# The first product on x times g, scaled by token afterwards, and a new order of the first loads, in a two-layer mLSTM and attention trunk

## The chip, the cores and the metric

The kernel runs on one core of a Trainium2 chip. The metric is the device time of one execution in microseconds. Before the change three runs gave 887.74, 888.80 and 890.71 us, a median of 888.8.

## The reference

Two layers over 256 tokens of 1024 channels, all in float32. Each layer computes, with x the running sum:

```python
h = rmsnorm(x, norm_mix_g[l])           # x * rsqrt(mean(x*x) + eps) * g
x = x + mixer_block(h, w_in[l], ...)    # proj = h @ w_in, split into mqk, mv, mo, gates, aq, ak, av, ga, gb
h = rmsnorm(x, norm_mlp_g[l])
x = x + sqrelu_mlp(h, w_up[l], w_down[l])
```

and at the end one more rmsnorm. Every projection starts from the same normed h; mv, the values of the mLSTM branch, is one of them: `mv = rmsnorm(x, g) @ w_in[:, 1024:2048]`. The norm's factor belongs to a token (a row of x) and g to a channel (a column).

## The kernel before, in words

Tokens lie in two tiles of 128 (tt = 0, 1) and channels in two halves of 512 (hf = 0, 1) or eight groups of 128 (k = 0 to 7). X holds x with tokens on the partitions. A product needs x transposed, with channels on the partitions (hT), so x is normed, transposed on TensorE against `ident`, and evacuated from PSUM.

Every matrix operand is split in two: hi, a rounded copy made by ScalarE, and lo, the remainder, made by VectorE as the operand minus hi. Each product is then three matmuls: hi by hi, hi by lo, lo by hi (`xs` at lines 202 to 215 with 512 output columns, `ws` at 217 to 229 with 256).

**Weights.** They come as pieces of 128 rows by 1024 columns (512 KB), loaded by SP (`piece`, line 89; `kv_piece`, lines 98 and 99, takes two loads for a piece) into four `raw` buffers. `pump_hi` (line 142) makes hi on ScalarE, `pump_lo` (line 117) makes lo on VectorE, and behind each lo `pump_dma` issues the load of the piece four further on, which takes the buffer that this lo has finished with. SP works in order: a load that waits for its buffer holds up all loads behind it.

**Slots.** The work of TensorE is a list of slots, each a list of units (three matmuls, or a call). `run_slots` (line 182) goes through them and emits for each slot, in this order: the functions of `at`, hi of the pieces that the slot may reach ahead to (four ahead of its own, `AHEAD`, or fewer by `limits`), the functions of `at_late`, the matching lo, the functions of `at_last`, the units, and the functions of `after`. Each engine works through its own instructions in the order in which they are emitted; what runs early or late is thus fixed by where it is emitted.

**The start.** Slots 0 to 7 are the product mv (`s_mv` = 0): piece k is used in slot k in the second half, and in slots 0 to 3 the order is "t", token tile 0 for k = 0, 1, then 2, 3, then token tile 1. Slots 8 to 11 (`s_kv` = 8) are the keys, values and gates, from pieces 8 to 11. `mv_evac` (lines 588 to 594) empties mv's four PSUM banks after slot 7: banks (tt, 0) on ScalarE, banks (tt, 1) on VectorE. The next product's banks (kk for the keys, kv0 and kv1 for values and gates) are the same ones: in the trace the first matmul of kk waits for ScalarE's first evacuation and the first of kv1 for VectorE's first.

`setup_start` (line 391) issues the first loads, all from SP: x of tile 0 in halves (lines 393, 394), the row of g (395), pieces 0 to 2, x of tile 1 (398), piece 3, and then eleven small loads (`small_loads`, line 379: the bias table, and for each layer gate biases, sinks, and the rows of the convolution). Then it emits warm-up matmuls on zeros (`N_WARM`). `first_norm` (line 515) squares x (lines 333, 335), forms the factor r (line 339 on VectorE, the power on POOL at line 340), scales (523), transposes (528), and evacuates hi and lo with g as a factor per partition (532, 538). The rest of x is done by `tr_all` from within slots 1 and 2.

`setup_small` runs at the head of slot 2: mask and constants on POOL, `Rs` (line 424) and `sel` (line 428) on ScalarE. `setup_cols` runs at the head of slot 4: TensorE transposes the 80 rows of the convolution weights and biases (line 432) and the bias table (435), VectorE copies them to `cw` and `rbT` (433, 437), POOL spreads the bias table.

Of the kernel before, what the change touches and what calls it, by code (L numbers as in the profile page):

```python
# [42 lines left out]
def trunk(ctx: ExitStack, tc: tile.TileContext, x, norm_mix_g, w_in, conv_w, conv_b, b_igate, b_fgate,  # L43
# [60 lines left out]
    def pump_dma():  # L104
        j = n_dma[0]
        if j < len(pieces):
            raws[j] = wp.tile([P, 1040], F32, tag="raw", bufs=N_RAW, name=nm("raw"))
            pieces[j][0](raws[j])
            n_dma[0] += 1
# [3 lines left out]
    def pump_lo(eng=None):  # L113
# [5 lines left out]
        los.clear()  # L119

# [110 lines left out]
    def call(f):  # L231
        return ([], f)
# [144 lines left out]
    N_WARM = (26, 16, 8)  # L377

    def small_loads():
        S0["b8"] = big8()  # L380
        rows = S0["rows"] = S0["b8"][:80, 0, 0:P]
        rb = S0["rb"] = const.tile([NB_BUCKETS, 16], F32, name="rb")
        nc.sync.dma_start(rb, rel_bias)
        for l in range(DEPTH):
            nc.sync.dma_start(gb_bias[:, l, 0:4], b_igate[l].partition_broadcast(P))
            nc.sync.dma_start(gb_bias[:, l, 4:8], b_fgate[l].partition_broadcast(P))
            nc.sync.dma_start(sink[:, l, :], attn_sinks[l].partition_broadcast(P))
            nc.sync.dma_start(rows[40 * l : 40 * l + 32, :], conv_w[l].rearrange("j (m c) -> (j m) c", c=P))
            nc.sync.dma_start(rows[40 * l + 32 : 40 * l + 40, :], conv_b[l].rearrange("(m c) -> m c", c=P))

    def setup_start():
        grow = big8()[:8, 0, 0:P]
        nc.sync.dma_start(X[:, 0, 0:512], xv[:, 0, 0:512])
# [13 lines left out]
        pw = psA()  # L407
        for _ in range(N_WARM[0]):
            nc.tensor.matmul(pw[:, :P], mask, mask, start=True, stop=True)
        pg = psA()  # L410
        nc.tensor.transpose(pg[:, :8], grow, ident[:8, :8])
        S0["gcol"] = const.tile([P, KT], F32, name="gcol")
        S0["pg"], S0["pw"] = pg, pw
        for _ in range(N_WARM[1]):
            nc.tensor.matmul(pw[:, :P], mask, mask, start=True, stop=True)
# [99 lines left out]
    def first_norm(st, xtag, nxt):  # L515

        xh, xl = st["hT"] = xT_tiles(xtag)
        N = [Norm(0), Norm(1)]
        gcol, xn, pts = S0["gcol"], {}, {}

        def scale(tt, hf):
            xn[tt, hf] = tmp()
            nc.vector.tensor_scalar(xn[tt, hf], X[:, tt, hc(hf)], N[tt].r[:, :1], None, op0=ALU.mult)

        def tr(tt, hf):
            pts[tt, hf] = psB()
            for j in range(4):
                nc.tensor.transpose(pts[tt, hf][:, j * P : (j + 1) * P], xn[tt, hf][:, j * P : (j + 1) * P], ident)

        def hi(tt, ks):  # L530
            for k in ks:
                nc.scalar.activation(xh[:, k, tt * P : (tt + 1) * P], pts[tt, k // 4][:, k % 4 * P : (k % 4 + 1) * P],  # L532
                                     AF.Copy, scale=gcol[:, k : k + 1])

        def lo(tt, ks):
            for k in ks:
                s = slice(tt * P, (tt + 1) * P)
                nc.vector.scalar_tensor_tensor(xl[:, k, s], pts[tt, k // 4][:, k % 4 * P : (k % 4 + 1) * P],
# [562 lines left out]
```

## Time and profile before

| what | value |
|---|---|
| median of three runs | 888.8 us |
| the profiled execution, its own time | 888.86 us |
| its span, first to last instruction | 887.0 us |
| TensorE matmuls busy | 872.7 us of the span |
| VectorE busy | 573.1 us |
| ScalarE busy | 467.2 us |
| mean granted TensorE clock | 0.997 |
| data moved by DMA | 155.28 MB, 175 GB/s |

Times in the profile are microseconds from the start of the span. A row of the timeline gives start, duration, engine, line of the kernel, operation, what it writes and reads, and in square brackets how long the engine sat idle before it and who released it. PE is TensorE, PEld its weight loads, DVE VectorE, ACT ScalarE, POOL GpSimd; SPq is the queue from which SP issues loads. A row of a table of stretches gives the stretch, its length, the busy time of each engine with the count of instructions, the granted clock as a share of full speed, the share of the DMA engines' time, and GB/s. Rows of one tile give the count and the least, median and largest duration in nanoseconds.

### The profile page before, as it was taken

The numbers are of one execution on the slowest core, as the hardware profiler recorded it, in microseconds if no ns is written. First come the engines' busy times: TensorE is split into PE (matmuls) and PEld (weight loads), VectorE is DVE, ScalarE is ACT, GpSimd is POOL, SyncE is SP. The second block draws the span as 40 slices with busy tenths as digits, with TensorE's granted clock in tenths as the row PEclk, the third lists the DMA queues.
The fourth block names the chain that finished last, engine by engine and source line by source line (L and its number), as shares of the span: only waits on it lengthen the run. The fifth ranks groups of instructions, "written<-read, shape, count | busy, mean of one in ns | idle before, by whom it ended". The sixth has DMA issues, their size and how long they took to land.

```text
span 887.0 us, 14892 instructions
## 1 busy us (share of the span) xinstructions
PE 872.7 (98%) x5837; PEld 788.0 (89%) x5837; DVE 573.1 (65%) x922; ACT 467.2 (53%) x769; POOL 132.3 (15%) x166
## 2 busy tenths in 40 slices
PE   8999999999999999999999999999999999999996
PEld 6899889999988999998889988899998899999985
DVE  5758879666666664545564778876666765737362
ACT  5556776654445454545355448665543553636351
POOL 1362434120000000000002435321100000000000
PEclk9999999999999999999999999999999999999999
DMA  6874435445457647474655545354464467565621
GB/s 229 280 259 169 139 119 167 142 145 169 163 190 236 208 146 239 128 247 138 202 180 178 171 139 154 133 146 163 143 216 147 159 217 236 168 211 173 201 104 48
DMA packets 48663, 155.28 MB, mean 175 GB/s; under 512 B 7912, under 2 KB 10064, under 8 KB 48592
## 3 DMA queue, kind: packets, MB, share of 16 engines
q1 hardware_dynamic: 47408, 150.63, 52.8%
q0 software_dynamic: 896, 3.17, 1.1%
q8 instruction: 46, 0.75, 0.3%
q10 hardware_dynamic: 288, 0.52, 0.2%
q14 instruction: 25, 0.20, 0.1%
HBM read 153.23 MB, written 1.07 MB: 174 GB/s over the span
## 4 chain that ended last, share of the span: by engine, by line
PE 90%; DVE 4%; DMA 2%; issue 2%; ACT 1%; POOL 0%; SPq 0%; POOLq 0%; ACTq 0%
PE pa L211 13%; PE pa L212 13%; PE pa L213 13%; PE pa L226 9%; PE pa L225 9%; PE pa L227 9%; PE pb L226 5%; PE pb L225 5%; PE pb L227 5%; DMA raw<-in_w_in 2%; PE pb L841 1%; PE pb L861 1%; DVE lo L117 1%; PE pb L313 1%; PE pb L901 1%
## 5 line engine op out<-in xcount | busy, mean ns | idle before, releaser
L117 DVE TENSOR_TENSOR lo<-raw,hi 128x1024 fp32r<-128x1024 f32 (+1 forms) x274 | 329.4, 1224 | 143.8 <-ACT hi L142 140.8
L142 ACT CAST hi<-raw 128x1024 fp32r<-128x1024 f32 (+1 forms) x280 | 286.6, 1049 | 187.4 <-PE pa L213 51.7
L225 PE MATMUL pa<-xh,hi 128*128 128x256 f32 x800 | 228.9, 286 | 0.6 <-ACT vm L594 0.6
L226 PE MATMUL pa<-xl,hi 128*128 128x256 f32 x800 | 225.5, 282 | 0.0
L227 PE MATMUL pa<-xh,lo 128*128 128x256 f32 x800 | 224.4, 281 | 0.0
L211 PE MATMUL pa<-hi,xh 128*128 128x512 f32 (+1 forms) x416 | 162.6, 391 | 0.7 <-ACT xh L532 0.6
L212 PE MATMUL pa<-lo,xh 128*128 128x512 f32 (+1 forms) x416 | 160.8, 387 | 0.6 <-DVE lo L117 0.4
L213 PE MATMUL pa<-hi,xl 128*128 128x512 f32 (+1 forms) x416 | 160.4, 386 | 0.0
L225 PEld LDWEIGHTS pa<-xh,hi 128*128 128x128 f32 x800 | 151.3, 189 | 1.7 <-ACT vm L594 1.1
L226 PEld LDWEIGHTS pa<-xl,hi 128*128 128x128 f32 x800 | 151.6, 189 | 0.3
L227 PEld LDWEIGHTS pa<-xh,lo 128*128 128x128 f32 x800 | 151.7, 190 | 0.0
L225 PE MATMUL pb<-xh,hi 128*128 128x256 f32 x384 | 108.2, 282 | 0.0
L226 PE MATMUL pb<-xl,hi 128*128 128x256 f32 x384 | 107.6, 280 | 0.0
L227 PE MATMUL pb<-xh,lo 128*128 128x256 f32 x384 | 107.4, 280 | 0.0
L212 PEld LDWEIGHTS pa<-lo,xh 128*128 128x128 f32 x416 | 78.3, 188 | 16.7 <-DVE lo L117 1.6
L213 PEld LDWEIGHTS pa<-hi,xl 128*128 128x128 f32 x416 | 78.1, 188 | 16.8
L211 PEld LDWEIGHTS pa<-hi,xh 128*128 128x128 f32 x416 | 78.2, 188 | 15.9 <-ACT xh L532 0.8
L340 POOL TENSOR_TENSOR sm<-sm,mhalf 128x1 f32<-128x1 f32 x10 | 7.4, 744 | 504.8 <-DVE sm L339 504.8
L226 PEld LDWEIGHTS pb<-xl,hi 128*128 128x128 f32 x384 | 72.4, 188 | 1.8
L225 PEld LDWEIGHTS pb<-xh,hi 128*128 128x128 f32 x384 | 72.2, 188 | 1.8
L227 PEld LDWEIGHTS pb<-xh,lo 128*128 128x128 f32 x384 | 72.2, 188 | 0.0
L211 PE MATMUL pa<-hi,b 128*128 128x512 f32 x128 | 50.4, 394 | 0.0
(197 smaller groups left out, 990.9 us busy)
## 6 DMA issues: line engine op xcount, KB each, us to landing
raw<-in_w_in SPq DMA_DIRECT2D x104, 512.0 KB, 4.4
raw<-in_w_up SPq DMA_DIRECT2D x64, 512.0 KB, 5.0
raw<-in_w_down SPq DMA_DIRECT2D x64, 512.0 KB, 4.4
raw<-in_w_branch_a SPq DMA_DIRECT2D x16, 512.0 KB, 3.5
raw<-in_w_branch_m SPq DMA_DIRECT2D x16, 512.0 KB, 3.8
raw<-in_w_out SPq DMA_DIRECT2D x16, 512.0 KB, 4.5
b<-ed SPq DMA_DIRECT2D x4, 512.0 KB, 4.9
g<-in_mlstm_norm_g POOLq DMA_DIRECT2D x2, 512.0 KB, 5.4
```

The source lines that it names most:

```text
L117: (eng or nc.vector).tensor_tensor(lo[:, :n], raw[:, :n], hi[:, :n].bitcast(F32), op=ALU.subtract)
L142: nc.scalar.copy(hi[:, :n], raw[:, :n])
L211: nc.tensor.matmul(b, xh[:, kt, s], wh[:, c], start=first, stop=False)
L212: nc.tensor.matmul(b, xh[:, kt, s], wl[:, c], start=False, stop=False)
L213: nc.tensor.matmul(b, xl[:, kt, s], wh[:, c], start=False, stop=last)
L225: nc.tensor.matmul(o, wh[:, c], xh[:, kt, :], start=first and half == 0, stop=False, skip_group_check=True)
L226: nc.tensor.matmul(o, wh[:, c], xl[:, kt, :], start=False, stop=False, skip_group_check=True)
L227: nc.tensor.matmul(o, wl[:, c], xh[:, kt, :], start=False, stop=last, skip_group_check=True)
L313: nc.tensor.transpose(pt[:, j * P : (j + 1) * P], src[:, j * P : (j + 1) * P], ident)
L841: nc.tensor.transpose(tp[:, j * P : (j + 1) * P], L[:, j * P : (j + 1) * P], ident)
L861: nc.tensor.matmul(o, va[:, 0, vs], PT[:, 0:T], start=(h0 % 4 == 0), stop=False, skip_group_check=True)
L901: nc.tensor.matmul(pn[:, :257], W[:, tt * P : (tt + 1) * P], vm[:, 0, h, :], start=True, stop=(tt == 0))
```

## The change

- The first product mv of layer 0 takes x times g, not normed (`hU`, in the tiles `xb`), and `mv_evac` multiplies its result by r, the norm's factor of each token.
- x is transposed as it is; VectorE multiplies by g out of PSUM into a buffer `xg` (`times_g`), ScalarE copies to hi, VectorE forms lo. Half 0 of both token tiles is done ahead of slot 0, half 1 within slots 1 and 2 (`rest`), and there, behind it, the squares and r too.
- The normed x for all later products (`hT`) is made from `xg` in slots 5 and 6: r is spread over all partitions by two small matmuls (`rows`), and `normed` multiplies and splits, four channel groups at a time.
- First loads: the row of g and x of tile 1, half 0, are issued by ScalarE; pieces 0 and 1 come in two halves each; x's second halves come before pieces 2 and 3. Piece 0 is also split in halves on ScalarE (`pump_hi_part`).
- The small loads go from the start to the ends of the preparation of slots 1, 2 and 3 (`at_last`), and the two layers' loads are merged.
- Slots 0 to 3 are in order "k" (piece k in slot k), slot 0 with token tiles inside. `limits` now holds slots 0 and 1 only. The warm-up matmuls are 24 and 22.

```diff
     def piece(w, kt, c0):
-        def load(raw):
-            nc.sync.dma_start(raw[:, :1024], w[kt * P : (kt + 1) * P, c0 : c0 + 1024])
+        def load(raw, parts=1):
+            for a in range(0, 1024, 1024 // parts):
+                b = a + 1024 // parts
+                nc.sync.dma_start(raw[:, a:b], w[kt * P : (kt + 1) * P, c0 + a : c0 + b])
...
+    def pump_hi_part(a, b):
+        j = n_split[0] - (1 if a else 0)
+        if not a:
+            pc[j] = tuple(wp.tile([P, 1040], F32R, tag=t, bufs=N_SPL, name=nm(t)) for t in ("hi", "lo"))
+            los.append(j)
+            n_split[0] += 1
+        nc.scalar.copy(pc[j][0][:, a:b], raws[j][:, a:b])
...
-    N_WARM = (26, 16, 8)
+    N_WARM = (24, 22)
...
+    def small_loads(i):
+        if i == 0:
+            S0["b8"] = big8()
+            S0["rows"] = S0["b8"][:80, 0, 0:P]
+            rb = S0["rb"] = const.tile([NB_BUCKETS, 16], F32, name="rb")
+            nc.sync.dma_start(rb, rel_bias)
+            nc.sync.dma_start(S0["rows"][0:64, :], conv_w.rearrange("l j (m c) -> (l j m) c", c=P))
+        elif i == 1:
+            nc.sync.dma_start(S0["rows"][64:80, :], conv_b.rearrange("l (m c) -> (l m) c", c=P))
+            nc.sync.dma_start(sink, attn_sinks.partition_broadcast(P))
+        else:
+            nc.sync.dma_start(gb_bias[:, :, 0:4], b_igate.partition_broadcast(P))
+            nc.sync.dma_start(gb_bias[:, :, 4:8], b_fgate.partition_broadcast(P))
 
     def setup_start():
         grow = big8()[:8, 0, 0:P]
+        nc.scalar.dma_start(grow, norm_mix_g[0].rearrange("(k c) -> k c", c=P))
         nc.sync.dma_start(X[:, 0, 0:512], xv[:, 0, 0:512])
+        nc.scalar.dma_start(X[:, 1, 0:512], xv[:, 1, 0:512])
+        pump_dma(2)
+        pump_dma(2)
         nc.sync.dma_start(X[:, 0, 512:], xv[:, 0, 512:])
-        nc.sync.dma_start(grow, norm_mix_g[0].rearrange("(k c) -> k c", c=P))
-        for i in range(N_RAW):
-            if i == 3:
-                nc.sync.dma_start(X[:, 1, :], xv[:, 1, :])
-            pump_dma()
-        small_loads()
+        nc.sync.dma_start(X[:, 1, 512:], xv[:, 1, 512:])
+        pump_dma()
+        pump_dma()
...
     def first_norm(st, xtag, nxt):
...
+        uh, ul = st["hU"] = xT_tiles("xb")
+        xg = big8((P, KT, T))
...
+        def times_g(tt, hf):
+            nc.vector.tensor_tensor(xg[sl(tt, hf)], pts[tt, hf].rearrange("p (k t) -> p k t", k=4),
+                                    gcol[:, 4 * hf : 4 * hf + 4].unsqueeze(2).to_broadcast([P, 4, P]), op=ALU.mult)
+
+        def hi(tt, hf):
+            nc.scalar.copy(uh[sl(tt, hf)], xg[sl(tt, hf)])
+
+        def lo(tt, hf):
+            nc.vector.tensor_tensor(ul[sl(tt, hf)], xg[sl(tt, hf)], uh[sl(tt, hf)].bitcast(F32), op=ALU.subtract)
+
+        pg = psA()
+        nc.tensor.transpose(pg[:, :8], S0["grow"], ident[:8, :8])
+        nc.vector.tensor_copy(gcol, pg[:, :8])
         tr(0, 0)
+        tr(1, 0)
+        for _ in range(N_WARM[1]):
             nc.tensor.matmul(S0["pw"][:, :P], mask, mask, start=True, stop=True)
+        times_g(0, 0)
+        hi(0, 0)
+        times_g(1, 0)
+        pump_hi_part(0, 512)
+        lo(0, 0)
+        hi(1, 0)
         pump_lo_part(0, 512)
+        lo(1, 0)
+        pump_hi_part(512, 1024)
         pump_lo_part(512, 1024)
         pump_lo_done()
         pump_hi(0, 1)
         pump_lo()
+
+        def rest(tt):
+            tr(tt, 1)
+            times_g(tt, 1)
+            hi(tt, 1)
+            lo(tt, 1)
+            N[tt].square(0)
+            N[tt].square(1)
+            N[tt].rstd()
+
+        u = slots[nxt][0]
+        u[1], u[2] = u[2], u[1]
+        limits[nxt] = 1
+        limits[nxt + 1] = 3
+        for tt in range(2):
+            slots[nxt + 1 + tt][0].insert(2, call(lambda tt=tt: rest(tt)))
+        S0["r"] = [lambda tt=tt: N[tt].r[:, :1] for tt in range(2)]
+
+        def rows():
+            pr = psB()
+            for tt in range(2):
+                nc.tensor.matmul(pr[:, tt * P : (tt + 1) * P], N[tt].r[:, 0:1].to_broadcast([P, P]), ident, start=True,
+                                 stop=True, skip_group_check=True)
+            S0["R"] = tmp()
+            nc.scalar.copy(S0["R"][:, 0:T], pr[:, 0:T])
+            st["hT"] = xT_tiles(xtag)
+
+        def normed(c):
+            s = (slice(None), slice(4 * c, 4 * c + 4), slice(None))
+            nc.vector.tensor_tensor(xg[s], xg[s], S0["R"][:, 0:T].unsqueeze(1).to_broadcast([P, 4, T]), op=ALU.mult)
+            evac_split(xg[s], st["hT"][0][s], st["hT"][1][s])
+
+        at(nxt + 5, rows)
+        at(nxt + 5, lambda: normed(0))
+        at(nxt + 6, lambda: normed(1))
+        for i in range(3):
+            at_last(nxt + 1 + i, lambda i=i: small_loads(i))
...
-        s_mv = xs_group(st, "mv", "hT", w, MV0, head="t")
+        s_mv = xs_group(st, "mv", "hT" if l else "hU", w, MV0, head="t" if l else "k")
...
+            if l == 0:
+                r = S0["r"][tt]()
+                if hf:
+                    nc.vector.tensor_scalar(o, i, r, None, op0=ALU.mult)
+                else:
+                    nc.scalar.activation(o, i, AF.Copy, scale=r)
+            elif hf:
...
         def cwc(j, m):
-            return cw[:, 40 * l + j * 8 + m : 40 * l + j * 8 + m + 1]
+            c = 32 * l + j * 8 + m if j < 4 else 64 + 8 * l + m
+            return cw[:, c : c + 1]
```

`setup_small` (head of slot 2) and `setup_cols` (head of slot 4) stay where they were.

More of the change, by code (lines that the diff above doesn't have):

```diff
@@ L102, in kv_piece, with pump_dma @@
         return len(pieces) - 1
-    def pump_dma():
+    def pump_dma(*parts):
         j = n_dma[0]
@@ L107, in pump_dma @@
             raws[j] = wp.tile([P, 1040], F32, tag="raw", bufs=N_RAW, name=nm("raw"))
-            pieces[j][0](raws[j])
+            pieces[j][0](raws[j], *parts)
             n_dma[0] += 1
@@ L406, in setup_start @@
         nc.vector.memset(mask, 0.0)
-        pw = psA()
+        pw = S0["pw"] = psA()
         for _ in range(N_WARM[0]):
             nc.tensor.matmul(pw[:, :P], mask, mask, start=True, stop=True)
[L410 to L415, printed above, removed]
+        S0["grow"] = grow
     def setup_small():
```

64 lines of the change are left out of this document (6 added, 58 removed).

## The prediction

> **What bounds the kernel now.** I read the engine totals first, then two long stretches, then the queues one by one over the first 37 us.
>
> ```profile
> PE 872.7 (98%) x5837; PEld 788.0 (89%) x5837; DVE 573.1 (65%) x922; ACT 467.2 (53%) x769; POOL 132.3 (15%) x166
> ```
> ```profile
> 0.00:37.00 37.00, 32.88 (x179) 25.38 (x180) 23.26 (x46) 23.46 (x43) 11.34 (x33) 1.00 0.72 242
> 37.00:887.00 850.00, 839.84 (x5660) 762.58 (x5659) 549.80 (x877) 443.78 (x727) 120.97 (x133) 1.00 0.54 172
> ```
> In the second fence the second number is the length of the stretch and the next five are busy us of PE, PEld, DVE, ACT and POOL. TensorE is busy 839.84 of 850 us after 37 us. Everything there follows TensorE's order, so a shift of the work at 37 us shifts the end by the same amount. The change touches only the first eight slots (one slot per 128 rows of weight in the product mv) and its price can be read where the next product starts. I measure everything at one matmul: the first of bank kv1 (L211, below at 36.36), which waits for VectorE to empty mv's bank (0,1).
>
> ```profile
> 8.03 0.50 PE L211 MATMUL pa<-hi,xh 128*128 128x512 f32 x1 [0.64 <-ACT xh L532]
> 22.70 0.23 PE L432 MATMUL pb<-ident,b 80*128 80x80 f32 x1
> 22.99 0.51 PE L211 MATMUL pa<-hi,xh 128*128 128x512 f32 x1
> 33.94 0.40 PE L213 MATMUL pa<-hi,xl 128*128 128x512 f32 x1
> 34.97 0.39 PE L225 MATMUL pa<-xh,hi 128*128 128x256 f32 x1 [0.63 <-ACT vm L594]
> 36.36 0.39 PE L211 MATMUL pa<-hi,xh 128*128 128x264 f32 x1
> ```
> The columns are start, duration, engine, line. L432 is the transposition of the convolution rows (setup_cols), at the head of slot 4; nothing is waited for there. The 48 matmuls of slots 4 to 7 run from 22.99 to 33.94, so one takes (33.94 - 22.99)/47 = 0.233 us.
>
> **The queues before.**
>
> ```profile
> 3.33 0.63 ACT L333 ACTIVATE tmp<-X 128x512 f32<-128x512 f32 x1 [1.10 <-DMA X<-in_x]
> 10.83 0.63 ACT L333 ACTIVATE tmp<-X 128x512 f32<-128x512 f32 x1
> 11.98 0.19 ACT L333 ACTIVATION_READ_ACCUMULATOR tmp<-X 128x1 f32 x1
> 12.14 1.05 ACT L142 CAST hi<-raw 128x1024 fp32r<-128x1024 f32 x1
> 15.57 0.53 ACT L424 CAST Rs<-tmp 128x384 fp32r<-128x384 f32 x1
> 16.61 0.19 ACT L428 CAST sel<-tmp 128x4 fp32r<-128x4 f32 x1 [0.52 <-POOL tmp L426]
> 19.65 1.05 ACT L142 CAST hi<-raw 128x1024 fp32r<-128x1024 f32 x1 [2.84 <-DMA raw<-in_w_in]
> 29.08 1.06 ACT L142 CAST hi<-raw 128x1040 fp32r<-128x1040 f32 x1 [1.52 <-DMA raw<-in_w_in]
> 31.38 1.06 ACT L142 CAST hi<-raw 128x1040 fp32r<-128x1040 f32 x1 [1.24 <-DMA raw<-in_w_in]
> 33.37 1.06 ACT L142 CAST hi<-raw 128x1040 fp32r<-128x1040 f32 x1 [0.92 <-DMA raw<-in_w_in]
> 34.33 1.07 ACT L594 COPY vm<-pa 128x512 f32<-128x512 f32 x2
> ```
> ```profile
> 12.25 0.21 DVE L339 TENSOR_SCALAR sm<-sm 128x1 f32<-128x1 f32 x1
> 20.73 1.22 DVE L117 TENSOR_TENSOR lo<-raw,hi 128x1024 fp32r<-128x1024 f32 x1 [3.60 <-ACT hi L142]
> 25.32 3.51 DVE L117 TENSOR_TENSOR lo<-raw,hi 128x1024 fp32r<-128x1024 f32 x3
> 35.62 1.28 DVE L592 COPY vm<-pa 128x512 f32<-128x512 f32 x2
> ```
> ```profile
> L465 DVE TENSOR_TENSOR X<-X,pa x12: 675/679/687, 255.9 to 698.4; 128x512 f32<-128x512 f32 x12
> ```
> ```profile
> 12.54 0.73 POOL L340 TENSOR_TENSOR sm<-sm,mhalf 128x1 f32<-128x1 f32 x1 [6.83 <-DVE sm L339]
> 13.51 0.77 POOL L423 MEMSET tmp<- 128x512 f32 x1
> ```
> ```profile
> 13.47 0.32 SPq L389 DMA_DIRECT2D b<-in_conv_b  x1
> 21.98 0.38 SPq L98 DMA_DIRECT2D raw<-in_w_in  x1
> 25.18 0.37 SPq L98 DMA_DIRECT2D raw<-in_w_in  x1
> 26.56 0.37 SPq L98 DMA_DIRECT2D raw<-in_w_in  x1
> 26.97 0.46 SPq L99 DMA_DIRECT2D raw<-in_w_in  x1
> ```
> Weight piece 3 is in at 12.14. The last convolution row is issued at 13.47, ahead of piece 4 in SP's queue and nine microseconds before TensorE wants it. Piece 8 is issued at 21.98, right after the lo of piece 4 (20.73 + 1.22) gave its buffer back. That order is what the change turns round.
>
> **The change, part by part.** *First product without the norm, halves loaded first.* Square, rstd and scaling leave the start; a transposition, times_g (VectorE out of PSUM, 0.68 by the L465 row), a copy on ScalarE (0.63) and a first half piece (0.63 at most) come in. Its four transpositions take 0.66:
>
> ```profile
> 6.28 0.66 PE L528 MATMUL pb<-ident,tmp 128*128 128x128 f32 x4 [0.63 <-DVE tmp L523]
> ```
> With x's first half in at 3.33, and 0.7 for the second half's 0.26 MB ahead of the half piece (at the 357 GB/s below), the first matmul can stand at 3.33 + 0.7 + 0.66 + 0.68 + 0.63 + 0.63 = 6.6, call it 6.7, instead of 8.03. I give this gain no value in the forecast, because TensorE then waits at slot 4 for longer than it gained. At nothing, for the same reason, go the two loads issued by ScalarE (its first work on data, at 3.33, waits for x anyway), pieces 0 and 1 in two halves, the other warm-up counts, the merged small loads and the new columns of cw. If that wait did not exist, a late second half of x would cost its own delay, some 0.8 for the two issues at 0.4.
>
> *The norm moved into slots 1 and 2.* rest(0) puts times_g, hi, lo, two squares and rstd behind the splits of pieces 2 and 3 on ScalarE and VectorE. setup_small (slot 2) now stands behind rest(0): its POOL work behind the power of rstd, and its two ScalarE copies Rs and sel ahead of the split of piece 4. Step by step:
> - Piece 3 is in at 11.6. As many bytes go ahead of it as before (12.14), but the lull around 4 us, where the gain row stood in SP's queue, goes to ScalarE's queue: 116 GB/s for one microsecond after 357.
>
> ```profile
> 2.50:3.50 1.00, 1.00 (x13) 1.00 (x11) 0.00 (x0) 0.17 (x1) 0.00 (x0) 1.00 0.99 357
> 3.50:4.50 1.00, 0.47 (x6) 0.30 (x4) 0.46 (x1) 0.55 (x2) 0.00 (x0) 1.00 0.54 116
> ```
> - hi of piece 3 1.05, lo 1.22: 13.9. times_g 0.68, copy 0.63, two squares 1.34 (10.83 to 12.17): 16.6. rstd's sum 0.29: 16.9. Power and z 1.82 (12.46 to 14.28): 18.7. Rs 0.53, then to sel's end 0.70 (16.10 to 16.80): 20.0.
> - hi and lo of piece 4, 2.30 from the start of one to the end of the other (19.65 to 21.95): 22.3. lo 5 and 6 at 1.17 each (3.51/3): 24.6.
>
> *The small loads moved behind pieces 6 and 7, 8 to 10, and 11.* conv_b (small_loads(1)) is issued at the end of slot 2, in SP's order behind pieces 8, 9 and 10, and these wait for lo 4, 5 and 6. Piece 10 needs 0.88 for its two issues (26.56 to 27.43): conv_b goes out at about 25.5. Before it in the rings: piece 8, issued at 22.3, lands 3.9 later as piece 9 did before (25.18 to 29.08), then two more at 2.15 each (29.08, 31.38, 33.37). So conv_b lands at 30.6. The bounds come from small loads of before (issue to landing is the last number), 4.5 and 6.3 after 25.5, that is 30.0 and 31.8:
>
> ```profile
> gb_bias<-in_b_fgate SPq DMA_DIRECT2D x2, 2.0 KB, 4.5
> sink<-in_attn_sinks SPq DMA_DIRECT2D x2, 8.0 KB, 6.3
> ```
> I take 30.6, since the pieces ahead of it are the nearest thing to it.
>
> *Slot 4.* TensorE gets there near 19 (first matmul 6.7, 48 x 0.233 = 11.2, two groups of transpositions and k = 0's waits another 1 to 2) and stands before the transposition of the rows for some 11 us. Behind it on its queue is the whole rest of the kernel; behind the copy of that transposition stand lo 8 and everything later on VectorE, and the bias copies on POOL, which slots 5 to 11 hide since the bias is first loaded at slot 12. Its clock falls, too:
>
> ```profile
> 522.00:525.00 3.00, 1.17 (x9) 0.81 (x8) 2.69 (x12) 0.51 (x1) 0.00 (x0) 1.00 0.59 175
> 525.90:529.30 3.40, 3.40 (x18) 3.40 (x17) 2.37 (x9) 2.02 (x7) 2.42 (x2) 0.51 0.02 5
> ```
> After three microseconds with 1.17 us of work, the clock (the third number from the end) was 0.51 for 3.4 us. I charge that once: 1.7 us lost; bounds none and twice. setup_cols 0.3 (22.70 to 22.99) and slot 4's 12 x 0.233 = 2.8 take 3.1 + 1.7 = 4.8: 35.4.
>
> *The normed x in slots 5 and 6.* It is new work of VectorE: per half of the channels a product (1.22 by the 128x1024 row; not shown in this type, so between 1.1 and 1.3) and a lo 1.22, with a hi of 1.05 on ScalarE between them. It begins with rows(): two small matmuls behind slot 4 (0.3, as the transpositions of setup_cols) and one copy (0.53 at most, as Rs): 36.3. Then product, hi, lo (3.5): 39.8. lo 9 1.17: 41.0. The second half: 44.5. lo 10 and 11: 46.9. From the start of the bank's emptying to kv1 0.74 (35.62 to 36.36): 47.6. On ScalarE: hi of the second half ends at 43.3, hi 10 and 11 2.1, the first evacuation 0.6 (34.33 to the keys at 34.97): 46.0; from the keys' first matmul to kv1 1.4 (34.97 to 36.36): 47.4. VectorE is the later. What the evacuations pay for their new factor (1.07 is the time of two without it) is within this rounding.
>
> **The sum.** 47.6 - 36.36 = 11.2 us later, and nothing after it gives time back. The profiled execution took 888.86 us with a span of 887.0, as good as the median of 888.8: 888.86 + 11.2 = 900.1.
>
> **The rivals.** *conv_b is not last.* If it lands before about 26, slot 4 is held by VectorE's own row: lo 6 at 24.6, times_g 25.3, copy and squares 27.3, hi and lo of piece 7 29.6, then the two column copies and lo 8 31.1, the two halves of the norm and lo 9 39.3, lo 10 and 11 41.7, kv1 42.4. That is 6.0 us later than 36.36: 894.9. For it speaks that nothing in the traces shows a small load behind three pieces; against it the order in SP's queue.
>
> ```profile
> 0.73 0.39 SPq L393 DMA_DIRECT2D X<-in_x  x1
> ```
> *conv_b does not queue.* If a small load passes the pieces ahead of it, it lands as fast as x's first half did (issued 0.73, used at 3.33, so 2.6): 28.1, and the sum is 2.5 us less, 897.6. The two landing rows speak against it: small loads with less ahead of them took 4.5 or more. The Trainium skill, page "DMA: Bandwidth & Descriptors", section "Anatomy of one DMA — SWDGE (gpsimd) path", goes this way: about 2.0 us fixed plus the bytes at 436 GB/s, measured for loads from GpSimd. By that rule, an estimate, conv_b would be in at 27.5 and the sum 897.0; those landing rows do not agree with it.
>
> *It does what its order suggests, and is faster.* The mechanism: TensorE starts 1.3 us earlier and finds every operand in slots 1 to 7, so that the 96 matmuls take 96 x 0.233 = 22.4, two groups of transpositions 1.3 and setup_cols 0.3: from 6.7 to 30.7, instead of 34.2 (33.94 + 0.23). That is 3.5 us with the same evacuation behind it: 885.4. It decides at one point: conv_b must be in before 19, so lo 6 done by 14; by my chain lo 3 alone ends at 13.9. It would need the splits to run some 10 us ahead of these rows.
>
> *It cancels out:* the wait at slot 4 is only as long as the head start, 888.9.
>
> By the Trainium skill, page "TensorE: Matmul & The Clock Gate", section "Why this matters for your kernels", the clock falls after a gap of about 3 us without matmuls. In the row above no gap can have been longer than 1.83 us and it fell all the same, so a second stall, of 1.9 us between mv's end (35.4 + 0.3 + 36 x 0.233 = 44.1) and the first key matmul (46.0), may cost another 1.7 us by the row, 901.8, and nothing by the page.
>
> **How the numbers follow.** Forecast (slot 4 waits for conv_b behind the pieces) 0.64; conv_b without queueing 0.10; conv_b not last 0.12; faster 0.09; cancels out 0.05. The time is the forecast's, 900.1. The range goes down to the case of conv_b not last with piece 3 one microsecond earlier (893.9) and up to the forecast with a second drop of the clock and piece 3 one microsecond later (900.1 + 1.7 + 1.0 = 902.8, rounded to 903.0); it leaves out faster and no change, 0.14, and little above. Over 0.3% (2.7 us, about what a measurement of this kernel can tell) faster 0.09, within it 0.05, slower 0.86.
>
> **What would show it.** Right: a gap of TensorE of 8 us or more ahead of the rows' transposition, ended by the convolution load; clock near 0.5 behind it; the splits of pieces 4 to 6 behind sel at about 20; kv1 near 47.6. Wrong: TensorE goes through slot 4 without a gap, or conv_b lands before 26, or the product mv ends before 34.

## The result and the profile after

Four runs of the changed kernel gave 898.50 to 901.02 us, median 900.13; the kernel before gave 888.71 in the same comparison (four runs, 887.74 to 890.71). The ratio is 1.0125, 95% interval 1.0108 to 1.0142: 11.4 us slower. The profiled execution is the slowest of the four, 901.02 us with a span of 899.2.

First the engine totals of the changed kernel, and two stretches of it, cut at 48 us instead of 37. Columns as in the prediction's fence.

```profile
PE 877.1 (98%) x5837; PEld 793.8 (88%) x5837; DVE 577.3 (64%) x913; ACT 467.9 (52%) x762; POOL 129.0 (14%) x166
```
```profile
0.00:48.00 48.00, 35.83 (x179) 29.32 (x180) 27.02 (x37) 24.36 (x36) 7.70 (x33) 0.89 0.60 198
48.00:899.00 851.00, 841.29 (x5660) 764.48 (x5659) 550.28 (x877) 443.56 (x726) 121.30 (x133) 1.00 0.53 171
```

The counts of the long stretch are those of before from 37 us (5660 matmuls in both), and it lasts 851 us instead of 850. So nearly the whole price was paid in the first 48 us, where the mean clock was 0.89 instead of 1.00. Now where TensorE waited longest, then the rows of its timeline at those places:

```profile
PE pb L440 <- DMA sink<-in_attn_sinks: 8.4, 1, 8.4
PE pa L235 <- ACT vm L623: 1.7, 1, 1.7
PE pb L536 <- DMA X<-in_x: 0.7, 1, 0.7
```
```profile
5.68 1.12 PE L536 MATMUL pb<-ident,X 128*128 128x128 f32 x4 [0.65 <-DMA X<-in_x]
6.59 2.55 PE L557 MATMUL pa<-mask 128*128 128x128 bf16 x22
8.90 0.78 PE L221 MATMUL pa<-hi,xh 128*128 128x512 f32 x1
30.01 0.36 PE L440 MATMUL pb<-ident,b 80*128 80x80 f32 x1 [8.43 <-DMA sink<-in_attn_sinks]
34.83 0.60 PE L592 MATMUL pb<-ident,sm 128*128 128x128 f32 x4
45.42 0.39 PE L235 MATMUL pa<-xh,hi 128*128 128x256 f32 x1 [1.66 <-ACT vm L623]
47.15 0.39 PE L221 MATMUL pa<-hi,xh 128*128 128x264 f32 x1 [0.39 <-DVE vm L621]
```

L440 is the transposition of the convolution rows (L432 before), L592 the spreading of the norm's factor, L235 the first key matmul, and the last row the first matmul of kv1, at 47.15 instead of 36.36. Two things in these rows mislead. The releaser of L440 is named as the load of the sinks, but L440 reads only the convolution rows; the convolution load was issued just ahead of it, and conv_first below shows that this load is the one waited for. And the first product starts later than before (8.90 against 8.03), not earlier.

SP's queue and ScalarE show why the load was late:

```profile
24.24 0.37 SPq L100 DMA_DIRECT2D raw<-in_w_in  x1
24.65 0.47 SPq L101 DMA_DIRECT2D raw<-in_w_in  x1
25.17 0.86 SPq L397 DMA_DIRECT2D b<-in_conv_b  x1
26.07 0.47 SPq L398 DMA_DIRECT2D sink<-in_attn_sinks  x1
```
```profile
11.79 1.05 ACT L152 CAST hi<-raw 128x1024 fp32r<-128x1024 f32 x1 [0.20 <-DMA raw<-in_w_in]
16.64 0.19 ACT L343 ACTIVATION_READ_ACCUMULATOR tmp<-X 128x1 f32 x1
19.54 0.19 ACT L436 CAST sel<-tmp 128x4 fp32r<-128x4 f32 x1 [0.52 <-POOL tmp L434]
19.64 2.93 ACT L152 CAST hi<-raw 128x1024 fp32r<-128x1024 f32 x3
44.69 1.26 ACT L623 ACTIVATE vm<-pa,sm 128x512 f32<-128x512 f32 x2
```

The load was issued at 25.17, behind both halves of piece 10. Before, it went out at 13.47. The hi of pieces 4 to 6 stands behind sel, at 19.64. On VectorE the rows after the gap are the two normed halves (L600, L315) and the splits between them:

```profile
20.72 3.50 DVE L119 TENSOR_TENSOR lo<-raw,hi 128x1024 fp32r<-128x1024 f32 x3 [3.51 <-ACT hi L152]
35.93 1.23 DVE L600 TENSOR_TENSOR b<-b,tmp 128x1024 f32<-128x1024 f32 x1 [4.02 <-ACT tmp L595]
40.57 1.22 DVE L600 TENSOR_TENSOR b<-b,tmp 128x1024 f32<-128x1024 f32 x1
42.90 1.23 DVE L315 TENSOR_TENSOR xl<-b,xh 128x1024 fp32r<-128x1024 f32 x1 [1.12 <-ACT xh L314]
44.04 2.39 DVE L119 TENSOR_TENSOR lo<-raw,hi 128x1040 fp32r<-128x1040 f32 x2
46.35 1.41 DVE L621 TENSOR_SCALAR vm<-pa,sm 128x512 f32<-128x512 f32 x2
```

Last the granted clock, third number from the end, in three stretches:

```profile
26.00:30.00 4.00, 0.00 (x0) 0.02 (x1) 1.63 (x3) 2.60 (x5) 0.92 (x2) 0.50 0.66 209
30.00:33.00 3.00, 2.99 (x8) 2.31 (x9) 1.50 (x3) 0.00 (x0) 2.11 (x10) 0.50 0.67 176
47.00:50.00 3.00, 2.85 (x14) 2.85 (x15) 3.00 (x4) 1.88 (x2) 0.00 (x0) 0.57 0.87 306
```

It was at half in the gap and for 3.7 us behind it, and fell a second time at 47.4, after the 1.66 us stall at the keys. This second stretch lasted to 50.8.

To follow the shift through the kernel I took the start of the same matmul in two traces and subtracted. The table has this shift against before, in us, at five places, given in before's time; "end" is the last matmul. The experiments below stand in it too.

```
kernel           36.36    41     88    100    520    535    end
after            10.8   12.3   12.5   12.7   12.9   11.8   12.1
conv_first        6.7    8.2    8.4    8.7    8.9    8.8    8.9
small_late        8.3    9.8   10.0   10.6   10.8   10.9   11.0
keep_clock        9.2    9.2    9.4    9.5    9.7    7.6    7.8
no_renorm         8.2    8.1    9.3   10.7   11.4    9.2    9.9
before_small      2.8    4.3    4.3    4.7    4.7    2.5    2.7
conv_small        2.6    4.2    4.4    4.4    4.7    3.7    3.9
rearranged       -0.1   -0.2    1.6    2.2    2.4    0.3    0.6
rearranged_x     -2.3   -2.3    1.3    3.3    3.5    1.3    1.6
rearranged_y      0.0    0.5    0.7    2.7    2.9    0.7    1.0
rearranged_z      6.0    7.4    7.9   10.0   10.1    7.9    8.1
```

Read the first line so: 10.8 by kv1, 1.5 more by 41 (the second drop of the clock), nearly nothing for the next 480 us, and 1.1 back at 525. There it is before's profiled execution that had a drop (the prediction's row of 525.90), while this one had none. So part of what a trace shows is the place where the clock happened to fall in that execution. Nor is the profiled execution always a median one: after's is 0.9 us above its median, and conv_first's 2.4 us.

### The profile page after: what moved, and what is told of

Same layout as the page of the kernel before. It is cut to its first block, busy times and chain, and to the rows that moved or that the text cites. A ratio compares the mean times of both kernels' runs of the same rounds, so it can differ in the third digit from the quotient of the medians.

```text
span 899.2 us, 14877 instructions
## 1 busy us (share of the span) xinstructions
PE 877.1 (98%) x5837; PEld 793.8 (88%) x5837; DVE 577.3 (64%) x913; ACT 467.9 (52%) x762; POOL 129.0 (14%) x166
## 4 chain that ended last, share of the span: by engine, by line
PE 87%; DVE 4%; issue 3%; DMA 2%; ACT 2%; POOL 1%; SPq 0%; POOLq 0%; ACTq 0%; DVEq 0%
PE pa L221 13%; PE pa L222 13%; PE pa L223 13%; PE pa L235 8%; PE pa L236 8%; PE pa L237 8%; PE pb L236 5%; PE pb L235 5%; PE pb L237 5%; DMA raw<-in_w_in 2%; DVE lo L119 1%; PE pb L875 1%; PE pb L895 1%; PE pb L323 1%; PE pb L935 1%
## 5 line engine op out<-in xcount | busy, mean ns | idle before, releaser
L235 PE MATMUL pa<-xh,hi 128*128 128x256 f32 x800 | 228.8, 286 | 1.7 <-ACT vm L623 1.7
L235 PEld LDWEIGHTS pa<-xh,hi 128*128 128x128 f32 x800 | 151.1, 189 | 2.7 <-ACT vm L623 2.1
L235 PE MATMUL pb<-xh,hi 128*128 128x256 f32 x384 | 108.5, 283 | 0.0
L235 PEld LDWEIGHTS pb<-xh,hi 128*128 128x128 f32 x384 | 72.3, 188 | 1.7
```

The lines of the kernel that those rows point to most:

```text
L235: nc.tensor.matmul(o, wh[:, c], xh[:, kt, :], start=first and half == 0, stop=False, skip_group_check=True)
```

## The experiments

Theory A is the prediction's: the convolution load (conv_b) stands behind piece 10, piece 10 behind the splits that setup_small and the moved norm hold up, and TensorE behind conv_b. The rivals were that VectorE's added work alone sets the time (B), and that the load of the sinks, which the profile names, is the one waited for (C).

**conv_first: the convolution load early, the sinks left where they are.**

```diff
         if i == 0:
...
+            nc.sync.dma_start(S0["rows"][64:80, :], conv_b.rearrange("l (m c) -> (l m) c", c=P))
         elif i == 1:
-            nc.sync.dma_start(S0["rows"][64:80, :], conv_b.rearrange("l (m c) -> (l m) c", c=P))
             nc.sync.dma_start(sink, attn_sinks.partition_broadcast(P))
```

> The changed kernel with one load moved: the convolution's bias rows (conv_b) are issued right behind the convolution's weight rows in slot 1, ahead of pieces 8 to 10; the sinks' load stays where it was. Theory A (slot 4 waits for conv_b behind these pieces): no gap in front of the rows' transposition; slot 4 is then held by lo 4 (21.9) and by x's last half (25.5), and VectorE's row sets the next product: lo 6 24.2, times_g, copy and squares 26.7, lo 7 28.9, lo 8 30.3, two halves of the norm with lo 9 38.4, lo 10 and 11 40.8, kv1 41.5 instead of 47.15, 5.6 us less: 894.5 (892.8 if the clock does not fall a second time). Theory B (VectorE's longer row is the bound and the gap only lies inside it): less than 1.5 us, 899 to 900. Theory C (the load waited for is the sinks', as the profile names it): the gap stays, ended near 29.9, 900.

Measured: 895.43 us (894.41 to 897.86), ratio 1.0082, interval 1.0065 to 1.0100, beside 888.11 for before. TensorE's timeline of this kernel:

```profile
23.04 0.23 PE L440 MATMUL pb<-ident,b 80*128 80x80 f32 x1
27.14 0.50 PE L221 MATMUL pa<-hi,xh 128*128 128x512 f32 x1 [2.10 <-ACT xh L546]
41.31 0.39 PE L235 MATMUL pa<-xh,hi 128*128 128x256 f32 x1 [3.15 <-ACT vm L623]
```

L440 has no wait at all now, and it runs before the sinks' load is even issued (26.79): C falls. By the medians 4.7 us of the 11.4 are gone, by the ratios 3.8 of 11.1, so B falls as the whole cause. Theory A's 894.5 is 0.9 below the measured time. What stays has two waits of its own: 2.10 us for x's last half (rest(1) stands behind the splits on ScalarE) and 3.15 us for the evacuation behind the normed halves. So the convolution load hid other late work, as the prediction's rival with conv_b not last had it.

**small_late: setup_small moved from slot 2 to slot 9.**

```diff
-            at(s_mv + 2, setup_small)
+            at(s_mv + 9, setup_small)
```

> The changed kernel with setup_small moved from slot 2 to slot 9, so that Rs and sel and the POOL work they wait for no longer stand ahead of the split of piece 4 on ScalarE. Theory A: hi 4 starts at 16.9 (end of the squares) instead of 19.64, and with it lo 4 to 6, pieces 8 to 10 and conv_b come 2.8 us earlier: conv_b in at 27.1, 897.3. A rival (the rings are the limit, so that pieces 8 to 10 and conv_b come no earlier): conv_b still near 29.9, 900.

Measured: 899.52 us (896.24 to 900.23), ratio 1.0125, interval 1.0103 to 1.0147. Theory A's 897.3 was missed, and the time alone says that nothing changed. Rows of ScalarE, SP and TensorE say otherwise:

```profile
17.19 2.93 ACT L152 CAST hi<-raw 128x1024 fp32r<-128x1024 f32 x3
```
```profile
22.70 0.86 SPq L397 DMA_DIRECT2D b<-in_conv_b  x1
```
```profile
27.35 0.37 PE L440 MATMUL pb<-ident,b 80*128 80x80 f32 x1 [5.30 <-DMA sink<-in_attn_sinks]
```

The splits start 2.45 us earlier than after's (19.64), conv_b goes out 2.47 earlier (25.17), L440 2.66 earlier (30.01): the chain from sel to the load is shown, link by link. In the table the shift against after's is 2.5 less at kv1 and 1.1 less at the end. Between 520 and 535 us 1.2 of the difference goes, because this execution had a drop of the clock near 537 and the profiled after had none, and 0.4 goes between 88 and 100 us. The medians differ by 0.6 only and the ratios not at all; what separates 0.6 from 1.1 is within the spread of four runs (896.24 to 900.23).

**keep_clock: matmuls on a constant in the gap, so that TensorE doesn't idle.**

```diff
     def setup_cols():
+        pd = psB()
+        for _ in range(135):
+            nc.tensor.matmul(pd[:, :P], identb, identb, start=True, stop=True)
```

> The changed kernel with 135 matmuls of 128 columns on the identity ahead of the rows' transposition in slot 4, about 7.6 us of work that nobody reads, inside the gap of 8.4 us. Theory A: the gap's end stays at 30.0, the clock stays at 1.00, setup_cols and slot 4 take 3.1 us instead of 4.8, and everything behind them comes 1.7 us earlier: 898.4. The rival (the slow clock is hidden behind VectorE's row): 900.1, unchanged.

Measured: 896.75 us (896.31 to 898.19), ratio 1.0104, interval 1.0089 to 1.0119. Two rows of TensorE's timeline and two stretches:

```profile
21.50 7.71 PE L441 MATMUL pb<-identb 128*128 128x128 bf16 x135
30.05 0.26 PE L443 MATMUL pb<-ident,b 80*128 80x80 f32 x1 [0.85 <-DMA sink<-in_attn_sinks]
```
```profile
30.00:33.00 3.00, 2.95 (x13) 2.40 (x14) 1.48 (x3) 0.00 (x0) 2.17 (x11) 1.00 0.69 178
47.00:50.00 3.00, 3.00 (x27) 3.00 (x26) 2.58 (x3) 1.44 (x2) 0.00 (x0) 1.00 0.84 254
```

The transposition still waits for its load until 30.05, and the clock is whole behind it: kv1 stands 1.6 us earlier than after's (9.2 against 10.8 in the table), the 1.7 that the prediction charged. The second drop is gone as well, though the stall that came before it is not (TensorE waited 1.7 us for ScalarE's evacuation here too): 3.1 us at 41. The medians differ by 3.4, the ratios by less (0.0021, or 1.9 us), with intervals that overlap. So the first drop cost its 1.7 us, and whether the second comes depends on more than the length of the stall just ahead of it (the last section has what the clock records show of this).

**no_renorm: the normed x left out.**

```diff
-        uh, ul = st["hU"] = xT_tiles("xb")
+        uh, ul = st["hU"] = xT_tiles(xtag)
...
-        at(nxt + 5, rows)
-        at(nxt + 5, lambda: normed(0))
-        at(nxt + 6, lambda: normed(1))
+        at(nxt + 5, lambda: st.update(hT=st["hU"]))
```

> The changed kernel without the normed x: rows() and normed() of slots 5 and 6 are left out and the later products of layer 0 read x times g as it is, so the norm's factor is missing from all of them but mv. Theory A: the gap at slot 4 stays as it is (ended at 30.0); mv ends at 43.4, the evacuations follow at once, kv1 at 45.3 instead of 47.15, and the second drop of the clock does not come: 1.85 + 1.7 less, 896.6. Theory B (VectorE's added work is what costs): most of the loss goes, 890 or less.

Measured: 898.28 us (896.46 to 899.23), ratio 1.0116, interval 1.0098 to 1.0133. The chief wait of TensorE, in the view of waits:

```profile
PE pb L440 <- DMA sink<-in_attn_sinks: 8.8, 1, 8.8
```

The gap stays, so B falls a second time; theory A's 896.6 was missed by 1.7 us. kv1 comes 2.6 us earlier and the second drop of the clock is missing, but between 41 and 100 us the shift grows from 8.1 to 10.7, where after's grew by 0.4. TensorE's waits there have two for VectorE that after's trace lacks: 0.6 us at L235 (for L679) and 1.2 us at L745 (for L735, the end of the scan of the gates). Why VectorE is late there stays open.

**before_small: the kernel before, with nothing but the small loads merged and issued late.** This takes the one part out of the change that the prediction blamed. The new `small_loads(i)` and the columns of cw are the change's own and are not shown again.

```diff
-        small_loads()
...
+        for i in range(3):
+            at_last(nxt + 1 + i, lambda i=i: small_loads(i))
```

> The kernel before with one part of the change alone: the merged small loads at the ends of the preparation of slots 1, 2 and 3, nothing else. The norm is still made at the start, so pieces ahead of conv_b go early. Theory A: piece 4 no longer stands behind the small loads, hi 4 starts after sel at 17, lo 4 ends at 19, and conv_b goes out behind piece 8 alone at 20; it lands at 24.5 while TensorE reaches slot 4 at 22.5: a gap of about 2 us, 890. The rival (the late place of the small loads alone makes the stall, whatever the splits do): a gap of 5 us or more, 894 or above. If the place does not matter at all: 888.

Measured: 892.31 us (891.89 to 893.85), ratio 1.0051, interval 1.0033 to 1.0069, beside 888.18 for before. Neither theory had it right. Rows of TensorE, SP and ScalarE, and a stretch:

```profile
24.07 0.29 PE L433 MATMUL pb<-ident,b 80*128 80x80 f32 x1 [0.17 <-DMA b<-in_conv_b]
37.72 0.39 PE L225 MATMUL pa<-xh,hi 128*128 128x256 f32 x1 [1.96 <-ACT vm L597]
```
```profile
21.30 0.46 SPq L387 DMA_DIRECT2D b<-in_conv_b  x1
23.89 0.37 SPq L98 DMA_DIRECT2D raw<-in_w_in  x1
25.34 0.47 SPq L391 DMA_DIRECT2D gb_bias<-in_b_fgate  x1
25.91 0.41 SPq L98 DMA_DIRECT2D raw<-in_w_in  x1
```
```profile
34.63 1.06 ACT L142 CAST hi<-raw 128x1040 fp32r<-128x1040 f32 x1 [5.84 <-DMA raw<-in_w_in]
```
```profile
28.00:31.00 3.00, 3.00 (x15) 2.47 (x14) 1.38 (x2) 0.78 (x1) 3.00 (x16) 1.00 0.27 49
```

The gap at the rows' transposition is 0.17 us, not 2: conv_b goes out behind piece 8 alone and lands within 2.8 us. The 4.1 us come elsewhere. The two loads of gate biases now stand between pieces 9 and 10. Piece 9, issued at 23.89, is split at 27.72. Piece 10, issued at 25.91 behind these loads, is in only at 34.63, ScalarE idles 5.84 us for it, and from 28 to 31 us only 49 GB/s move, against 287 before:

```profile
28.00:31.00 3.00, 3.00 (x15) 2.47 (x14) 1.66 (x2) 1.06 (x1) 3.00 (x13) 1.00 0.98 287
```

The evacuation, which stands behind these splits, then holds the keys up by 1.96, and the clock falls to 0.57 from 39 to 43 us. That the gate biases' loads cause the slow stretch is argued from their place; I did not move them alone. The packet records of the traces speak for it: the two loads are 512 packets of 16 bytes, and in all twelve traces, wherever the loads stand, these packets take 4.6 to 7.4 us from the first to the last. Over the middle four fifths of them all loads together move only 7 to 59 GB/s, though in each trace weight pieces were issued just before or meanwhile.

**conv_small: both edits together, the convolution load early (conv_first) and setup_small late (small_late).** Its edit is the two diffs shown above.

> The changed kernel with both edits at once: conv_b behind the convolution's weight rows in slot 1, and setup_small in slot 9. Theory A: no gap for a load at slot 4, and the splits of pieces 4 to 6 and VectorE's whole row 2.6 us earlier than with conv_b moved alone (895.4): 892.8. The rival (the order on ScalarE only mattered through conv_b's issue): 895.4.

Measured: 892.76 us (892.08 to 894.59), ratio 1.0054, interval 1.0038 to 1.0070. TensorE's timeline:

```profile
20.68 0.26 PE L440 MATMUL pb<-ident,b 80*128 80x80 f32 x1 [0.30 <-DMA b<-in_conv_b]
36.83 0.58 PE L235 MATMUL pa<-xh,hi 128*128 128x256 f32 x1 [3.21 <-ACT vm L623]
```

The gap is gone (L440 comes two microseconds ahead of before's 22.70), and the keys wait 3.21 us for the evacuation that stands behind the normed halves. By the medians the two edits together take 7.4 of the 11.4 us away, by the ratios 6.3 of 11.1. What is left fits the normed halves in front of the evacuation: the wait is 2.6 us longer than before's 0.63, and kv1 comes 2.6 us later. The drop of the clock behind that stall adds 1.6 (2.6 to 4.2 in the table).

**rearranged and rearranged_x: the same idea with the order mended.** In rearranged the small loads go out in slots 0 and 1, setup_cols runs in slot 6, setup_small in slot 9, both second halves of x in slot 1, the squares in slot 3, and the normed halves in slots 6 and 8. In rearranged_x the first half of x's second tile is issued by SP, too, and piece 1 comes in one load (the second part of the diff is rearranged_x's alone). The diff shows parts only.

```diff
-    N_WARM = (24, 22)
+    N_WARM = (24, 5, 8)
...
-        nc.scalar.dma_start(X[:, 1, 0:512], xv[:, 1, 0:512])
+        nc.sync.dma_start(X[:, 1, 0:512], xv[:, 1, 0:512])
         pump_dma(2)
-        pump_dma(2)
+        pump_dma()
...
+        limits[nxt + 5] = limits[nxt + 6] = 8
+        limits[nxt + 7] = 9
...
-        at(nxt + 5, rows)
-        at(nxt + 5, lambda: normed(0))
-        at(nxt + 6, lambda: normed(1))
+        at(nxt + 6, rows)
+        at(nxt + 6, lambda: normed(0))
+        at(nxt + 8, lambda: normed(1))
```

> The changed kernel put in another order, all of its computation kept: conv_w, conv_b and sinks issued in slot 0 and the gate biases in slot 1; setup_small in slot 9, setup_cols in slot 6; both halves 1 of x split in slot 1 and all four squares in slot 3; rows and the first half of the normed x in slot 6, its second half in slot 8; pieces 9 to 11 not split ahead of mv's evacuation, but for piece 9; warm-up matmuls 24, 5 and 8. Theory A: from the rows, lo 4 ends at 18.5 before TensorE reaches slot 4 near 20, R is there at 26.5, mv ends at 32, kv1 at 34.0 to 35 against 36.36 before: 886.5 to 887.5. Theory B (the second making of the norm costs its time on VectorE wherever it stands): 892 or more.

> The kernel rearranged with x of tile 1, half 0, issued by SP right behind tile 0's, and piece 1 in one load. Before, a second half of x issued second by SP was in at 4.0; issued by ScalarE in the changed kernel it was in at 5.7 to 6.5. So times_g of tile 1 comes 1.5 us earlier and the first product with it, unless the half piece behind it is the later: 0 to 1.5 us less than rearranged, 885.5.

Measured: rearranged 890.38 us (nine runs, 889.41 to 892.86), ratio 1.0023, interval 1.0009 to 1.0037; rearranged_x 889.41 us (ten runs, 888.33 to 891.20), ratio 1.0013, interval 1.0003 to 1.0023. Both miss their expectations. TensorE in rearranged_x:

```profile
6.83 0.50 PE L221 MATMUL pa<-hi,xh 128*128 128x512 f32 x1 [0.79 <-ACT hi L129]
32.54 0.39 PE L235 MATMUL pa<-xh,hi 128*128 128x256 f32 x1 [0.29 <-ACT vm L630]
46.95 0.39 PE L235 MATMUL pa<-xh,hi 128*128 128x256 f32 x1 [1.10 <-ACT tmp L655]
```

The start does all that the change could do: first matmul at 6.83 instead of 8.03, the keys at 32.54 instead of 34.97, kv1 2.3 us ahead. By the trace it is lost by 48 us: the splits of pieces 9 to 11, held back to make room for the normed halves, give their buffers back late, the next four pieces come late, and the evacuation of the keys and values (L655) stands on ScalarE behind their hi. ScalarE also idles 1.49 us for POOL ahead of sel (41.66), in front of the split of piece 12, since setup_small now stands there.

**rearranged_y and rearranged_z: is it the late buffers, or the added work wherever it stands?** Both are rearranged_x without its limits; in rearranged_z setup_small is in slot 5 and the second normed half in slot 7.

```diff
-        limits[nxt + 5] = limits[nxt + 6] = 8
-        limits[nxt + 7] = 9
```

> The last rearrangement (x of tile 1, half 0, issued by SP, piece 1 whole) without its limits on slots 5 to 7, so that the splits of pieces 9 to 11 are again emitted ahead of the normed halves. With the limits, kv started 2.4 us ahead of before and all of it was gone by 48 us, behind weight splits 12 to 15 whose loads wait for the buffers of pieces 9 to 11. Theory A, the late buffers are what gave the lead back: the lo of piece 11 ends near 37 instead of 41.6, the loads of pieces 12 to 15 go out about 3 us earlier, and TensorE at 48 us is 1.5 to 2.4 us ahead of before: 886 to 887. Theory B, what gives it back is the work that the normed x adds to VectorE (two products and two remainders, 4.9 us), wherever it stands: then kv itself starts about 2.4 us later, at 35.5, and the time is 888.5 to 890.

> As the kernel beside it, and setup_small at the head of slot 5 instead of slot 9 (its copy sel waited 1.5 us for POOL on ScalarE ahead of the split of piece 12), the second normed half at slot 7 instead of 8. Theory A: the stall of 1.5 us on ScalarE near 41 is gone, and TensorE at 48 us is 2 us or more ahead of before: 885.5 to 887. Theory B (the added work of VectorE): both orders give 888.5 to 890, with waits for VectorE at the keys or kv in place of those for ScalarE behind them.

Measured: rearranged_y 890.47 us (twelve runs, 888.84 to 892.30), ratio 1.0027, interval 1.0016 to 1.0037; rearranged_z 896.56 us (five runs, 894.86 to 897.38), ratio 1.0087, interval 1.0074 to 1.0100, beside 887.88 for before. The first key matmul of rearranged_y and the stretch behind it, then the same matmul of rearranged_z:

```profile
34.23 0.55 PE L235 MATMUL pa<-xh,hi 128*128 128x256 f32 x1 [1.89 <-ACT vm L628]
```
```profile
34.00:37.50 3.50, 3.27 (x15) 3.27 (x16) 3.50 (x5) 0.76 (x2) 3.18 (x9) 0.54 0.62 194
```
```profile
40.24 0.58 PE L235 MATMUL pa<-xh,hi 128*128 128x256 f32 x1 [7.82 <-ACT vm L628]
```

rearranged_y ends 0.5 us above theory B's range (888.5 to 890) and 3.5 above theory A's: with the splits ahead again, the evacuation is late and the keys wait 1.89 us, and the clock at 0.54 behind the stall takes the rest of the lead. In rearranged_z both theories miss: the second normed half is emitted in slot 7, ahead of mv's evacuation, and the keys wait 7.82 us. It changes two places at once, so it does not show what the wait for sel was worth. No order that I tried beats the kernel before.

## Why the prediction was right

It was right in its mechanism and in its time (900.1 against 900.13). That the two agree to 0.03 us is luck: the four runs spread over 2.5 us, and the profiled execution, 901.02, is 0.9 above the forecast. Point by point:

- *Pieces 3 to 6.* Piece 3 was split at 11.79 (11.6 forecast), the squares ended at 16.83 (16.6), sel at 19.73 (20.0), lo 6 at 24.22 (24.6). small_late shows that the step which orders them, setup_small behind the norm and ahead of the splits, costs 2.5 us of the load's delay.
- *conv_b.* Issued at 25.17 (25.5), its reader ran at 30.01 (30.6). The two ends of the bound were 4.5 and 6.3 us from issue to landing; by the profile's table of issues it took 4.7. In before_small, behind one piece instead of three, the reader ran 2.8 us after the issue: the time depends on what stands ahead, and the rival without queueing (in at 28.1) falls. The Trainium skill, page "DMA: Bandwidth & Descriptors", section "Anatomy of one DMA — SWDGE (gpsimd) path", gives about 2.0 us fixed for a load from GpSimd. These loads are issued by SP: before_small's 2.8 us is not far from that figure, and after's 4.7 is not covered by it.
- *The gap.* 8.4 us where 11 were forecast, since TensorE came to it 2.6 us later. Here a step failed, "the first matmul can stand at 6.7": it stood at 8.90. The prediction's sum left out what stands ahead of the product in TensorE's own order, the transpositions of x's second tile and the 22 warm-ups, and put the loads issued by ScalarE and the warm-up counts at nothing. The first half of x's second tile, issued by ScalarE, was in only at 5.68, and the transpositions and the warm-ups ran at half speed (1.12 us for four transpositions, 0.60 at 13.61; 2.55 us for the 22). The clock record of this trace begins with full speed only at 9.87, before's at 3.73. Nothing came of it, as it had said: the gap's end is set by the load. rearranged_x has the start at 6.83.
- *Slot 4.* From 30.01 to the next slot's L592 at 34.83 are 4.82 us, against 4.8 with one drop of the clock.
- *The normed halves.* R was done at 35.90 (36.3), the halves at 39.5 and 44.1 (39.8, 44.5), lo 11 at 46.43 (46.9), kv1 at 47.15 (47.6). The shift of 10.79 is 0.4 below the sum's 11.2.
- *"Charge the drop once".* The traces fell a second time, after the stall at the keys, which the prediction forecast as 1.9 us and which was 1.66. That made 12.3 by 41 us in the table. By the Trainium skill, page "TensorE: Matmul & The Clock Gate", section "Why this matters for your kernels", only a gap of more than about 3 us should do that; here the second drop came after a stall of 1.66 us, so the trace does not agree, and keep_clock, with a stall as long, had no drop. In layer 2 before's execution had a drop that the profiled after did not, and 1.1 came back. By its own terms, up to kv1, the forecast of 11.2 was 0.4 too high. The drop of 1.5 and the 1.1 that came back, which it left out of the sum, nearly cancel, so that the end is near it again: 12.1 in the profiled execution, 11.4 in the medians.
- *The rivals.* conv_b not last was priced at 894.9, and conv_first, which makes it so, took 895.43. It was not the case here. "Faster" needed conv_b before 19 and 885.4 us; with conv_b out of the way and the start at 6.83, rearranged_x still took 889.41. The rival left out that VectorE and ScalarE then have the normed halves to make in the same time, right where the evacuation and the next product's weights stand.

So of the 11.4 us the two places in the order, conv_b and setup_small, make 7.4 (conv_small, by the medians; 6.3 by the ratios). The rest goes with the order of the normed halves, the other moved work and the clock drop behind their stall, of which rearranged_x takes nearly all away. Leaving the norm out of the start saves 1.2 us at the first matmul and 2.3 at kv1, and that was given back in every order tried: at the keys, where the normed halves (4.9 us of VectorE, two products and two remainders) stand ahead of mv's evacuation, or behind them, where the weight splits that had to make room are late. Where rearranged_x loses more, between 88 and 100 us (1.3 to 3.3 in the table), its trace has the same wait of 1.2 us for the gates' scan as no_renorm's (L754 for L744), and behind it a half-clock stretch from 93.33 to 96.75; why VectorE comes late there stays open.

## What to carry to other kernels

When a small load is moved later, count what is ahead of it in its queue and what *those* wait for; here 8 KB behind three weight pieces held TensorE for 8.4 us, and issuing them earlier was worth about 4 us (4.7 by the medians, 3.8 by the ratios). Work that is taken off a start and done later has to find a place where no evacuation and no buffer return is queued behind it; a gain at the first matmul proves nothing until the start of the next product has been read as well. And where the clock drops at changing places, compare positions of the same instruction in two traces, not only times: small_late's 2.5 us are plain there and lost in the medians.

## What the runs showed of the hardware

- The half-clock stretches of TensorE cost some 1.7 us per 3.4 us and don't come at fixed places. The stall of 1.7 us at the keys was followed by one in after and by none in keep_clock, and near 530 us before, conv_first and small_late had one, while all other rows of the table go down there by 1.0 to 2.2 us.
- The clock records of the twelve traces say more. They change only on a grid of 3.41 us, which lies differently in each execution: half-clock stretches within the products last 3.41, 6.83 or 10.24 us. All 17 falls ahead of the end of the products followed a grid step in which matmuls were busy for 0.56 of the time or less. Only two such steps at full clock had no fall behind them (0.51 in keep_clock from 41.14, 0.52 in conv_first from 36.39). After's stall at the keys lies in the step from 44.00 to 47.41, with 1.60 us of matmuls. Near 530 before's step from 522.55 was busy for 0.55 and the clock fell; after's idle time at the same work is spread over steps of which the emptiest was busy for 0.70, and it did not fall. So it matters how much of one step a stall fills; what decides close to one half stays open.
- A 256 KB load of x issued by ScalarE at 1.33 took 4.3 us from issue to landing beside SP's weight loads. In rearranged_x the same load, issued by SP at 1.17 ahead of the weights, was used at 4.99. The runs don't separate the issuing engine from the place in the order: the three loads of x that SP issued in after took 4.1 us in the median.
- Matmuls that only warm the array delay a product when they run at half speed: 22 of them took 2.55 us in after (0.116 us each), where keep_clock's 135 took 7.71 (0.057 each).
- The releaser that the profile names for a wait on a load can be a neighbour of the true one: the sinks' load, issued 0.9 us behind conv_b, was named for L440, and in conv_first L440 ran at 23.04 without a wait, 3.7 us before the sinks' load was issued.
- In before_small the rate of all loads fell to 49 GB/s for three microseconds with weight pieces outstanding, behind two loads of 4 KB that go to all partitions in packets of 16 bytes. The same 512 packets take 4.6 us or more in every trace.
